# Hybrid DiT block: gated sum kept in its PSUM bank, second norm scaled by a diagonal in the turn, rows left unsplit until their sums

## The chip, the cores and the metric

One Trainium2 chip, one core. The metric is the device time of one execution of the kernel in microseconds (us); the time of a kernel is the median of its runs.

## The reference

One layer of a diffusion backbone on 1024 latent tokens of width 1024 with 256 context tokens, all in fp32. A recurrence branch (HGRN2) and a windowed attention branch read the same normalised input. Then:

```python
def _merge(y_hg, y_at, gates, w_bh, w_ba, w_o):
    g_hg, g_at = jnp.split(gates, 2, axis=-1)
    mixed = jax.nn.sigmoid(g_hg) * (y_hg @ w_bh) + jax.nn.sigmoid(g_at) * (y_at @ w_ba)
    return mixed @ w_o

def _rmsnorm(x, w):
    xf = x.astype(jnp.float32)
    y = xf * lax.rsqrt(jnp.mean(xf * xf, axis=-1, keepdims=True) + EPS)
    return (y * w.astype(jnp.float32)).astype(x.dtype)

def _modulate(x, w, shift, scale):
    return _rmsnorm(x, w) * (1.0 + scale) + shift

def _swiglu(h, w_gate, w_up, w_down):
    return (jax.nn.silu(h @ w_gate) * (h @ w_up)) @ w_down
```

The merged result, times a gate `g1`, is added to the tokens (x); x is normalised a second time (`_modulate`), goes through `_swiglu` with an inner width of 2816, and is added to x once more.

## The kernel before, in words

Large products run as three fp32r matmuls each: an operand is split into a high part (a cast to fp32r on ScalarE) and a low part (the difference, on VectorE), and high x high, high x low, low x high are summed in a PSUM bank of 128x512. All TensorE instructions are issued in program order by a helper (L76 for a matmul, L79 for a transpose); the order on the other engines is a scheduler's.

**Gated sum (L1159 to L1179).** For each of eight channel tiles `ct` the weights are loaded and split (L136, L137) and two gate rows `ga`, `gb` are loaded and put through a sigmoid. For each token half `t` GpSimd multiplies `gb` by the attention branch (L1169), TensorE makes `bh` of 12 matmuls (four k steps of three) in a bank of the two-bank pool `mm`, VectorE multiplies it by `ga` (L1173) and adds `gb` (L1174), both into `ga`, and the result is split into `mx` (L1175 on ScalarE, L1176 on VectorE).

**Out-projection (L1182 to L1197, L1309 to L1323).** Each half of the weights `wop` comes by DMA (L1188), is multiplied by `g1` on GpSimd (L1193), cast on ScalarE (L1194) and its low part made on VectorE (L1195). `project(nh, bs)` runs eight k steps of three matmuls for each block of 128 tokens in `bs`, yields after each step, and VectorE adds the bank to `xn` (L1323). The first half (nh = 0) runs for all eight blocks, then the second half block by block.

**Second norm (L1212 to L1224, L1266 to L1303).** After block b's second half, `second_norm(b)` squares both halves of `xn[b]` on ScalarE with the sum beside it (L1216, the squares land in `xh`), GpSimd adds the two sums, takes the mean and the root (L1219 to L1221), VectorE scales `xn` by it into `xh` (L1223), and SP stores the rows (L1224). `second_norm_t(b)`, "the turn", then transposes the eight 128x128 pieces of `xh` into two banks `tp` (L1279), and ScalarE applies scale and shift into `r` (L1282). It runs inside block b + 1's second projection, after six of its eight k steps (L1330); block 7's runs behind the first product of both FFN chains (L1483). For blocks 0 to 3 the two results are split into the FFN operands HB11 and HB21. For blocks 4 to 7 three differences and sums with the earlier blocks are made, the earlier rows being put together again from their two parts (L1294, L1295, L1300, L1301), and split into HT2, HT3, HB22; `kt` (from `keep`) holds two of the sums for later operands.

**FFN (L1397 on).** Seven products per pair of tiles replace eight (Strassen's scheme with Winograd's sums). `ux` is made in a bank of `mm` for even pairs: first with HB11, later with HT2; `uz` uses HB21. The weights' sums are made on VectorE in between (L1379 to L1386, L1461 to L1464).

Of the kernel before, what the change touches and what calls it, by code (L numbers as in the profile page):

```python
# [9 lines left out]
F32 = mybir.dt.float32  # L10
# [4 lines left out]
ALU = mybir.AluOpType  # L15
# [4 lines left out]
P = 128  # L20
# [23 lines left out]
def tile_hybrid_block(  # L44
# [1114 lines left out]
    for ct in range(KT):  # L1159
# [7 lines left out]
        for t in range(2):  # L1167
            a = slice(t * 512, t * 512 + 512)
            pool.tensor_tensor(gb[:, a], gb[:, a], t2[ct][t], ALU.mult)  # L1169
            mh, ml = mixed(t, 0, ct), mixed(t, 1, ct)  # L1170
            ps = mm_tile(f"bh_{ct}_{t}")
            whole(gemm_ch(ps, w, hg_hi[t], hg_lo[t], 4))
            dve.tensor_tensor(ga[:, a], ga[:, a], ps, ALU.mult)  # L1173
            dve.tensor_tensor(ga[:, a], ga[:, a], gb[:, a], ALU.add)  # L1174
            act.copy(mh, ga[:, a])  # L1175
            dve.tensor_tensor(ml, ga[:, a], mh.bitcast(F32), ALU.subtract)  # L1176
        if ct == 0:
# [32 lines left out]
    xn_d = [dram.tile([P, D], F32, name=f"xn_d{b}") for b in range(NB)]  # L1210

    def second_norm(b):  # L1212
        xh = []
        for u in range(2):
            xt = pt.tile([P, 512], F32, tag="tmp", bufs=4, name=f"xh{b}_{u}")
            act.activation(xt, xn[b][:, u * 512 : u * 512 + 512], AF.Square, accum_out=ss2[:, 2 * b + u : 2 * b + u + 1])  # L1216
            xh.append(xt)
        r = rs2[:, b : b + 1]
        pool.tensor_tensor(r, ss2[:, 2 * b : 2 * b + 1], ss2[:, 2 * b + 1 : 2 * b + 2], ALU.add)  # L1219
        pool.tensor_scalar(r, r, 1.0 / D, EPS, ALU.mult, ALU.add)  # L1220
        pool.tensor_tensor(r, r, mhalf[:, :1], ALU.pow)  # L1221
        for u in range(2):
            dve.tensor_scalar(xh[u], xn[b][:, u * 512 : u * 512 + 512], r, None, ALU.mult)  # L1223
        sp.dma_start(xn_d[b], xn[b])  # L1224
        return xh

# [22 lines left out]


    kept = {}

    def keep(nm, b):
        i = b % 4
        if i % 2 == 0:
            if (nm, i) == (1, 0):
# [8 lines left out]

    def second_norm_t(b, xh):  # L1266
        t, c = b // 4, slice((b % 4) * P, (b % 4) * P + P)
# [3 lines left out]
        if b == 4:  # L1271
            hop_tile(HT2, pn, ("n8", "n9"))
            hop_tile(HT3, pmA, ("a0", "a1"))
            hop_tile(HB22, pmA, ("a2", "a3"))
        dst = [quarter(pt.tile([P, 512], F32, tag="tmp", bufs=4, name=f"r{b}_{u}")) for u in range(2)]
        for u in range(2):
            tp = psF.tile([P, 512], F32, tag="tp", bufs=2, name=f"tp2_{b}_{u}")
            for i in range(4):
                pe.transpose(tp[:, i * P : i * P + P], xh[u][:, i * P : i * P + P], ident)  # L1279
            for i in range(4):  # L1280
# [5 lines left out]
        if t == 0:  # L1286
            return

        def f(o, p):
            return hop[o][p][:, :, c].bitcast(F32)  # L1290

        r12, r22 = dst
        t1, t4 = keep(1, b), keep(4, b)
        dve.tensor_tensor(t1, r12, f(HB11, 0), ALU.subtract)  # L1294
        dve.tensor_tensor(t1, t1, f(HB11, 1), ALU.subtract)  # L1295
        dve.tensor_tensor(t4, r22, t1, ALU.subtract)
        split_h(HT2, t4, c)
        dve.tensor_tensor(r12, r22, r12, ALU.subtract)
        split_h(HT3, r12, c)
        dve.tensor_tensor(t4, f(HB21, 0), t4, ALU.subtract)  # L1300
        dve.tensor_tensor(t4, t4, f(HB21, 1), ALU.add)  # L1301
        split_h(HB22, r22, c)
# [24 lines left out]
    def norm_late(gen):  # L1327

        for i, us in enumerate(gen):
            if i == 5 and late:  # L1330
                second_norm_t(*late.pop(0))
# [162 lines left out]
    for b in range(2, NB):  # L1494
        whole(project(0, (b,)))
    for b in range(NB):
        norm_late(project(1, (b,)))
        late.append((b, second_norm(b)))
# [153 lines left out]
```

## Time and profile before

| | |
|---|---|
| time, median of 3 runs (lowest to highest) | 1693.41 us (1687.12 to 1694.36) |
| profiled execution: its own time | 1698.77 us |
| its span, mean granted TensorE clock | 1697.0 us, 0.981 |
| busy: TensorE, VectorE, ScalarE, GpSimd | 1609.2, 1111.1, 758.7, 284.6 us |

PE is TensorE, PEld its weight loads, DVE VectorE, ACT ScalarE, POOL GpSimd, SP the engine that issues most DMAs. Busy times are sums of instructions with overlaps taken out; a time of one instruction on PE or DVE is longer than the distance between the starts of two that follow each other, since they are pipelined. The granted clock is a share of 2.4 GHz. L1173 is line 1173 of the kernel before; a name like `gt` is a tile, and `gt<-gt,bh` an instruction that writes `gt` from `gt` and `bh`.

### The profile page before, as it was taken

What the parts mean: (1) busy time and instruction counts of PE and PEld (TensorE: products, weight loads), DVE (VectorE), ACT (ScalarE), POOL (GpSimd) and SP (SyncE); (2) the same over time, 40 slices, a digit from 0 to 9 for tenths busy, and PEclk for the clock granted to TensorE, in tenths of its full rate; (3) what the DMA queues carried; (4) which work ended last, traced back from release to release, by engine and by line L of the source; (5) the groups of instructions that cost most, each with busy time, mean ns of one, the idle gap of its engine ahead of it and who ended that gap; (6) DMA issues with size and microseconds to landing.
All of it is one profiled execution on the core that took longest, in us unless ns stands there. A gap on an engine that the chain in (4) does not pass through costs nothing.

```text
span 1697.0 us, 23284 instructions
## 1 busy us (share of the span) xinstructions
PE 1609.2 (95%) x8424; PEld 1341.9 (79%) x8424; DVE 1111.1 (65%) x2018; ACT 758.7 (45%) x1405; POOL 284.6 (17%) x339
## 2 busy tenths in 40 slices
PE   6899999999899999999988997899999999999998
PEld 3689879998777787778877776687888888888887
DVE  3872577777768969696328628877555665646464
ACT  4411345555555565644445247333333333443431
POOL 2402454420012313132114412000000000000000
PEclk9899999999999999999999999899999999999999
DMA  9771312221366566552265414786233222577573
GB/s 361 269 268 52 106 60 69 67 94 54 127 192 202 188 204 202 200 171 93 87 218 183 160 50 149 275 293 219 99 110 126 94 99 100 195 241 239 189 235 123
DMA packets 199468, 274.18 MB, mean 162 GB/s; under 512 B 13775, under 2 KB 115248, under 8 KB 199352
## 3 DMA queue, kind: packets, MB, share of 16 engines
q1 hardware_dynamic: 183800, 250.13, 44.0%
q10 hardware_dynamic: 15552, 22.55, 3.6%
q8 instruction: 66, 1.08, 0.3%
q14 instruction: 50, 0.41, 0.1%
HBM read 192.14 MB, written 80.49 MB: 161 GB/s over the span
## 4 chain that ended last, share of the span: by engine, by line
PE 36%; DMA 5%; DVE 4%; ACT 2%; issue 2%; POOL 1%; SPq 0%; POOLq 0%; ACTq 0%; DVEq 0%
PE ux L76 10%; PE dx L76 7%; PE dy L76 5%; PE uy L76 5%; PE wo L76 3%; PE uz L76 3%; DMA wd<-in_w_ffn_down_dram 2%; PE ba L76 1%; ACT r L1282 1%; PE bh L76 1%; DMA gt<-gates_d 1%; DMA dr<-in_w_ffn_down_dram 1%; DMA wr<-in_w_ffn_up_dram 1%; ACT xh L1216 0%; DVE mx L1176 0%
## 5 line engine op out<-in xcount | busy, mean ns | idle before, releaser
L76 PE MATMUL ux<-hop,op 128*128 128x512 f32 x1032 | 244.2, 394 | 8.6 <-ACT hop L1240 4.4
L76 PEld LDWEIGHTS ux<-hop,op 128*128 128x128 f32 x1032 | 196.5, 191 | 51.1 <-ACT hop L1240 4.8
L1241 DVE TENSOR_TENSOR dp<-dr,dp 128x1024 fp32r<-128x1024 f32 x77 | 93.9, 1223 | 85.1 <-ACT dp L1240 77.6
L1240 ACT CAST dp<-dr 128x1024 fp32r<-128x1024 f32 x77 | 81.0, 1052 | 117.6 <-PE dy L76 49.1
L76 PE MATMUL uy<-hop,op 128*128 128x512 f32 x528 | 123.3, 389 | 0.0
L76 PE MATMUL dx<-dp 128*128 128x512 f32 x528 | 120.6, 389 | 0.6 <-DVE cu L1476 0.6
L76 PEld LDWEIGHTS dx<-dp 128*128 128x128 f32 x528 | 99.0, 188 | 21.6 <-DVE cu L1476 1.0
L76 PEld LDWEIGHTS uy<-hop,op 128*128 128x128 f32 x528 | 99.1, 188 | 20.6
L76 PE MATMUL g<-hhi,whi_g 128*128 128x512 f32 x256 | 110.7, 433 | 2.3 <-ACT gs_g L348 2.3
L76 PE MATMUL g<-hhi,wlo_g 128*128 128x512 f32 x256 | 101.5, 396 | 0.0
L76 PE MATMUL g<-hlo,whi_g 128*128 128x512 f32 x256 | 101.2, 395 | 0.0
L76 PE MATMUL wo<-wop,mx 128*128 128x512 f32 x384 | 90.4, 395 | 0.0
L76 PE MATMUL dy<-dp 128*128 128x512 f32 x396 | 90.2, 389 | 0.0
L76 PEld LDWEIGHTS dy<-dp 128*128 128x128 f32 x396 | 74.3, 188 | 15.4
L1241 DVE TENSOR_TENSOR op<-wr,op 128x512 fp32r<-128x512 f32 x84 | 57.6, 685 | 40.6 <-ACT op L1240 40.5
L76 PEld LDWEIGHTS wo<-wop,mx 128*128 128x128 f32 x384 | 72.4, 190 | 14.8
L1240 ACT CAST op<-wr 128x512 fp32r<-128x512 f32 x84 | 52.1, 623 | 68.0 <-PE ux L76 36.1
L1241 DVE TENSOR_TENSOR op<-ws,op 128x512 fp32r<-128x512 f32 x66 | 45.5, 689 | 42.8 <-ACT op L1240 42.5
L655 DVE CUSTOM_DVE_ANT_0 e<-s,masks,bc 128x640 f32<-128x640 f32 (+1 forms) x64 | 54.2, 848 | 27.1 <-PE s L76 26.8
L660 ACT ACTIVATE e<-e,ngm 128x640 f32<-128x640 f32 (+1 forms) x64 | 51.7, 808 | 38.5 <-DVE ngm L659 38.3
L678 ACT CAST th<-ptp 128x512 fp32r<-128x512 f32 x76 | 43.2, 587 | 45.7 <-PE ptp L79 43.6
L679 DVE TENSOR_TENSOR tl<-ptp,th 128x512 fp32r<-128x512 f32 x76 | 51.1, 687 | 15.2 <-ACT th L678 14.6
(458 smaller groups left out, 3940.1 us busy)
## 6 DMA issues: line engine op xcount, KB each, us to landing
aw<-in_w_ada_dram SPq DMA_DIRECT2D x24, 1024.0 KB, 9.1
dr<-a_d SPq DMA_DIRECT2D x77, 256.0 KB, 4.0
wr<-in_w_ffn_gate_dram SPq DMA_DIRECT2D x11, 1024.0 KB, 5.1
wd<-in_w_ffn_down_dram SPq DMA_DIRECT2D x22, 512.0 KB, 6.7
wr<-in_w_ffn_up_dram SPq DMA_DIRECT2D x11, 1024.0 KB, 6.2
t_d<-td SPq DMA_DIRECT2D x44, 256.0 KB, 2.1
a_d<-cu SPq DMA_DIRECT2D x44, 256.0 KB, 2.6
dr<-t_d SPq DMA_DIRECT2D x44, 256.0 KB
```

Of the source, the lines that this page charges most:

```text
L76: self.chain(nc.tensor.matmul(*a, **k))
L655: dve.tensor_tensor_reduce(e[:, :n], ps[:, LC : LC + n], self.mask, 1.0, sinkb[:, 4 * g + j : 4 * g + j + 1], ALU.add, ALU.max, self.mx[:, ...
L660: tbl(act.activation(e[:, :n], e[:, :n], AF.Exp, bias=self.ngm[:, j : j + 1], accum_out=self.den[:, j : j + 1]))
L678: self.copied = act.copy(th, tp)
L679: dve.tensor_tensor(tl, tp, th.bitcast(F32), ALU.subtract)
L1240: act.copy(hi, src)
L1241: dve.tensor_tensor(lo, src, hi.bitcast(F32), ALU.subtract)
L1282: act.activation(dst[u][:, i], tp[:, i * P : i * P + P], AF.Identity, scale=m2[:, 8 + m : 9 + m], bias=m2[:, m : m + 1])
```

## The change

Three parts. The gated sum runs in place in its bank, which now comes from the four-bank `gu` pool; its split reads the bank. The second norm scales by a matmul: the turn multiplies a piece of `xn` by a diagonal of the reciprocal roots (128x128, `diag`), where it transposed a scaled copy; the first square of a block is issued two blocks behind its first projection (those of blocks 6 and 7 behind the last one), the squares land in `mm` banks, and the turn is hooked one k step later. The turned rows of blocks 0 to 3 are written straight into the kept tiles, unsplit, and the sums of blocks 4 to 7 are made from these in place.

```diff
--- before.py
+++ after.py
@@ -1168,12 +1168,12 @@
             a = slice(t * 512, t * 512 + 512)
             pool.tensor_tensor(gb[:, a], gb[:, a], t2[ct][t], ALU.mult)
             mh, ml = mixed(t, 0, ct), mixed(t, 1, ct)
-            ps = mm_tile(f"bh_{ct}_{t}")
+            ps = psF.tile([P, 512], F32, tag="gu", name=f"bh_{ct}_{t}")
             whole(gemm_ch(ps, w, hg_hi[t], hg_lo[t], 4))
-            dve.tensor_tensor(ga[:, a], ga[:, a], ps, ALU.mult)
-            dve.tensor_tensor(ga[:, a], ga[:, a], gb[:, a], ALU.add)
-            act.copy(mh, ga[:, a])
-            dve.tensor_tensor(ml, ga[:, a], mh.bitcast(F32), ALU.subtract)
+            dve.tensor_tensor(ps, ps, ga[:, a], ALU.mult)
+            dve.tensor_tensor(ps, ps, gb[:, a], ALU.add)
+            act.copy(mh, ps)
+            dve.tensor_tensor(ml, ps, mh.bitcast(F32), ALU.subtract)
         if ct == 0:
             g1 = pt.tile([P, 1024], F32, tag="gg", bufs=1, name="g1")
             sp.dma_start(g1, mod2_d[0, 0:D].partition_broadcast(P))
@@ -1209,20 +1209,21 @@
     rs2 = const.tile([P, NB], F32, name="rs2")
     xn_d = [dram.tile([P, D], F32, name=f"xn_d{b}") for b in range(NB)]
 
+    def square(b, u):
+        act.activation(mm_tile(f"sq{b}_{u}"), xn[b][:, u * 512 : u * 512 + 512], AF.Square,
+                       accum_out=ss2[:, 2 * b + u : 2 * b + u + 1])
+
     def second_norm(b):
-        xh = []
-        for u in range(2):
-            xt = pt.tile([P, 512], F32, tag="tmp", bufs=4, name=f"xh{b}_{u}")
-            act.activation(xt, xn[b][:, u * 512 : u * 512 + 512], AF.Square, accum_out=ss2[:, 2 * b + u : 2 * b + u + 1])
-            xh.append(xt)
+
+        square(b, 1)
         r = rs2[:, b : b + 1]
         pool.tensor_tensor(r, ss2[:, 2 * b : 2 * b + 1], ss2[:, 2 * b + 1 : 2 * b + 2], ALU.add)
         pool.tensor_scalar(r, r, 1.0 / D, EPS, ALU.mult, ALU.add)
         pool.tensor_tensor(r, r, mhalf[:, :1], ALU.pow)
-        for u in range(2):
-            dve.tensor_scalar(xh[u], xn[b][:, u * 512 : u * 512 + 512], r, None, ALU.mult)
+        diag = pt.tile([P, 512], F32, tag="tmp", bufs=4, name=f"diag{b}")[:, :P]
+        dve.tensor_scalar(diag, ident, r, None, ALU.mult)
         sp.dma_start(xn_d[b], xn[b])
-        return xh
+        return diag
 
 
 
@@ -1248,11 +1249,12 @@
...
     kept = {}
 
     def keep(nm, b):
         i = b % 4
-        if i % 2 == 0:
+        if (nm, i) not in kept:
             if (nm, i) == (1, 0):
                 pg = pt.tile([P, 1024], F32, tag="gg", bufs=1, name=f"kt{nm}_{i}")
             elif (nm, i) == (4, 2):
@@ -1263,7 +1265,7 @@
             kept[nm, i + 1] = quarter(pg[:, 512:])
         return kept[nm, i]
 
-    def second_norm_t(b, xh):
+    def second_norm_t(b, diag):
         t, c = b // 4, slice((b % 4) * P, (b % 4) * P + P)
         if b == 0:
             hop_tile(HB11, pmB, ("b0", "b1"))
@@ -1272,11 +1274,15 @@
             hop_tile(HT2, pn, ("n8", "n9"))
             hop_tile(HT3, pmA, ("a0", "a1"))
             hop_tile(HB22, pmA, ("a2", "a3"))
-        dst = [quarter(pt.tile([P, 512], F32, tag="tmp", bufs=4, name=f"r{b}_{u}")) for u in range(2)]
+        t1, t4 = keep(1, b), keep(4, b)
+        dst = (t1, t4)
+        if t:
+            dst = [quarter(pt.tile([P, 512], F32, tag="tmp", bufs=4, name=f"r{b}_{u}")) for u in range(2)]
         for u in range(2):
             tp = psF.tile([P, 512], F32, tag="tp", bufs=2, name=f"tp2_{b}_{u}")
             for i in range(4):
-                pe.transpose(tp[:, i * P : i * P + P], xh[u][:, i * P : i * P + P], ident)
+                m = 4 * u + i
+                pe.matmul(tp[:, i * P : i * P + P], xn[b][:, m * P : m * P + P], diag, start=True, stop=True)
             for i in range(4):
                 m = 4 * u + i
                 act.activation(dst[u][:, i], tp[:, i * P : i * P + P], AF.Identity,
@@ -1285,20 +1291,14 @@
                 split_h((HB11, HB21)[u], dst[u], c)
         if t == 0:
             return
-
-        def f(o, p):
-            return hop[o][p][:, :, c].bitcast(F32)
-
         r12, r22 = dst
-        t1, t4 = keep(1, b), keep(4, b)
-        dve.tensor_tensor(t1, r12, f(HB11, 0), ALU.subtract)
-        dve.tensor_tensor(t1, t1, f(HB11, 1), ALU.subtract)
-        dve.tensor_tensor(t4, r22, t1, ALU.subtract)
-        split_h(HT2, t4, c)
+        t2_ = quarter(pt.tile([P, 512], F32, tag="tmp", bufs=4, name=f"t2_{b}"))
+        dve.tensor_tensor(t1, r12, t1, ALU.subtract)
+        dve.tensor_tensor(t2_, r22, t1, ALU.subtract)
+        split_h(HT2, t2_, c)
         dve.tensor_tensor(r12, r22, r12, ALU.subtract)
         split_h(HT3, r12, c)
-        dve.tensor_tensor(t4, f(HB21, 0), t4, ALU.subtract)
-        dve.tensor_tensor(t4, t4, f(HB21, 1), ALU.add)
+        dve.tensor_tensor(t4, t4, t2_, ALU.subtract)
         split_h(HB22, r22, c)
 
     def late_operands(o, nm):
@@ -1327,7 +1327,7 @@
     def norm_late(gen):
 
         for i, us in enumerate(gen):
-            if i == 5 and late:
+            if i == 6 and late:
                 second_norm_t(*late.pop(0))
 
 
@@ -1493,6 +1493,9 @@
     first_operands()
     for b in range(2, NB):
         whole(project(0, (b,)))
+        square(b - 2, 0)
+    square(NB - 2, 0)
+    square(NB - 1, 0)
     for b in range(NB):
         norm_late(project(1, (b,)))
         late.append((b, second_norm(b)))
```

VectorE, last two channel tiles of the gated sum, where the out-projection's weights (`wop`, L1195) come in between. Lines with - are before, with + after; `bh` is the bank, `gt` the gate rows, `mx` the low part of the split.

```order
 L1195 TENSOR_TENSOR wop_0_9679<-wo_0_9677,wop_0_9679 128x512
-L1173 TENSOR_TENSOR gt_9542<-gt_9542,bh_1_9566 128x512
+L1173 TENSOR_TENSOR bh_1_9566<-bh_1_9566,gt_9542 128x512
+L1176 TENSOR_TENSOR mx_1_1_9294<-bh_0_9548,mx_0_1_9292 128x512
+L1174 TENSOR_TENSOR bh_1_9566<-bh_1_9566,gt_9542 128x512
 L1195 TENSOR_TENSOR wop_0_9679<-wo_0_9677,wop_0_9679 128x512
-L1176 TENSOR_TENSOR mx_1_1_9294<-gt_9542,mx_0_1_9292 128x512
-L1174 TENSOR_TENSOR gt_9542<-gt_9542 128x512
```

The instructions now name the bank `bh` where they named `gt`, and L1176 and L1174 stand ahead of the second L1195 where they stood behind it.

TensorE, from the second half of block 6's turn to the FFN's first product. `tp_6_1` is the turn, `wo_7` block 7's out-projection, `ux_0` the FFN's first product. Before:

```order
L79 MATMUL tp_6_1_10461<-ident,xh_1_10423 128x128 [waits DVE_49,Activation_49]
L79 MATMUL tp_6_1_10461<-ident,xh_1_10423 128x128 x3
L76 MATMUL wo_7_10431<-wop_6_9755,mx_0_1_9296 128x512 x2
L76 MATMUL wo_7_10431<-wop_6_9755,mx_1_1_9298 128x512
L76 MATMUL wo_7_10431<-wop_6_9755,mx_0_1_9296 128x512 x2
L76 MATMUL wo_7_10431<-wop_6_9755,mx_1_1_9298 128x512
L76 MATMUL ux_0_10503<-hop_0_10062,ope_0_9839 128x512
L76 MATMUL ux_0_10503<-hop_1_10063,ope_0_9839 128x512
```

After:

```order
L76 MATMUL tp_6_1_10458<-diag_10422,xn_9722 128x128 [waits Activation_49]
L76 MATMUL tp_6_1_10458<-diag_10422,xn_9722 128x128 x3
L76 MATMUL wo_7_10425<-wop_6_9755,mx_0_1_9296 128x512 x2
L76 MATMUL wo_7_10425<-wop_6_9755,mx_1_1_9298 128x512
L76 MATMUL ux_0_10492<-hop_0_10079,ope_0_9839 128x512 [waits Activation_49]
L76 MATMUL ux_0_10492<-hop_1_10080,ope_0_9839 128x512
```

Three `wo_7` rows stand behind the turn where six stood, and the first `ux_0` has a wait on ScalarE that it had not.

VectorE, from the first sum of the FFN's weights (L1379) on, block 7. `xn_9724` is its residual (L1323), `kt` a kept tile, `hop` an operand's part. Before, up to L1323:

```order
L1379 TENSOR_TENSOR ws_10565<-wr_0_10563 128x512
L1300 TENSOR_TENSOR kt_0_10333<-hop_0_10064,kt_0_10333 128x512
L1294 TENSOR_TENSOR kt_2_10470<-r_0_10450,hop_0_10062 128x512
L1380 TENSOR_TENSOR ws_10565<-ws_10565,wr_0_10563 128x512
L1382 TENSOR_TENSOR wr_0_10563<-wr_0_10563 128x4x128
L1301 TENSOR_TENSOR kt_0_10333<-kt_0_10333,hop_1_10065 128x512
L1295 TENSOR_TENSOR kt_2_10470<-kt_2_10470,hop_1_10063 128x512
L1298 TENSOR_TENSOR r_0_10450<-r_1_10451,r_0_10450 128x512
L1323 TENSOR_TENSOR xn_9724<-xn_9724,wo_7_10431 128x512
```

After, up to block 7's diagonal (L1224 there):

```order
L1379 TENSOR_TENSOR ws_10553<-wr_0_10551 128x512
L1323 TENSOR_TENSOR xn_9724<-xn_9724,wo_7_10425 128x512
L1242 TENSOR_TENSOR hop_1_10607<-kt_0_10084,hop_0_10606 128x4x128
L1296 TENSOR_TENSOR kt_2_10197<-r_0_10447,kt_2_10197 128x512
L1242 TENSOR_TENSOR hop_1_10607<-kt_0_10084,hop_0_10606 128x4x128
L1380 TENSOR_TENSOR ws_10553<-ws_10553,wr_0_10551 128x512
L1382 TENSOR_TENSOR wr_0_10551<-wr_0_10551 128x4x128
L1297 TENSOR_TENSOR t_6_10467<-r_1_10448,kt_2_10197 128x512
L1299 TENSOR_TENSOR r_0_10447<-r_1_10448,r_0_10447 128x512
L1242 TENSOR_TENSOR hop_1_10316<-r_1_10448,hop_0_10315 128x4x128
L1224 TENSOR_SCALAR diag_10487<-ident,rs_9763 128x128
```

The residual stands second where it stood ninth. Before, 44 instructions stand from L1379 to the low part of block 7's HT2; after, 35.

## Rows read from the trace of the kernel before

**Rows 1.** Windows by stage: length, busy PE, PEld, DVE, ACT, POOL, clock, DMA share, GB/s.

```profile
919.60:938.50 18.90, 12.19 (x50) 8.87 (x49) 18.35 (x18) 10.13 (x15) 15.73 (x11) 1.00 0.61 192
938.50:991.40 52.90, 52.90 (x235) 43.80 (x235) 26.53 (x34) 11.09 (x20) 15.11 (x13) 1.00 0.34 113
991.40:1030.20 38.80, 33.61 (x169) 27.12 (x168) 16.99 (x29) 26.39 (x72) 7.25 (x15) 1.00 0.17 68
1030.20:1067.70 37.50, 24.20 (x98) 19.08 (x96) 35.92 (x62) 26.11 (x58) 6.48 (x6) 0.84 0.47 162
1075.00:1483.00 408.00, 405.70 (x1782) 335.13 (x1780) 266.09 (x414) 152.55 (x257) 0.00 (x0) 1.00 0.46 159
```

**Rows 2.** Waits of PE, 886 to 1075 us: us in total, times, longest.

```profile
PE tp L79 <- DVE xh L1223: 12.0, 7, 4.5
PE bh L76 <- DVE gt L1173: 6.7, 4, 2.7
PE ux L76 <- ACT hop L1240: 4.4, 1, 4.4
```

**Rows 3.** Timeline of PE: start, us, instruction [idle before <-releaser]; the branch and output products.

```profile
887.17 0.62 PE L76 MATMUL bh<-yh_s,whi_bh 128*128 128x512 f32 x2
...
938.55 53.21 PE L76 MATMUL wo<-wop,mx 128*128 128x512 f32 x234
```

**Rows 4.** Timeline of DVE, 917 to 948 us: first, last but one, last.

```profile
917.28 1.77 DVE L137 TENSOR_TENSOR wlo_bh<-wraw_bh,whi_bh 128x512 fp32r<-128x512 f32 x1
...
946.15 0.68 DVE L1195 TENSOR_TENSOR wop<-wo,wop 128x512 fp32r<-128x512 f32 x1
946.75 1.78 DVE L1176 TENSOR_TENSOR mx<-gt,mx 128x512 fp32r<-128x512 f32 x1
```

**Rows 5.** Tile gt: ns min/median/max, first and last start, form.

```profile
L1173 DVE TENSOR_TENSOR gt<-gt,bh x16: 672/677/689, 890.1 to 943.6; 128x512 f32<-128x512 f32 x16
L1174 DVE TENSOR_TENSOR gt<-gt x16: 676/684/1773, 890.9 to 944.3; 128x512 f32<-128x512 f32 x16
```

**Rows 6.** Windows of line L1195 alone: us, DVE busy (x count), clock, DMA share, GB/s.

```profile
917.28:948.54 31.26, 9.14 (x8) 1.00 0.62 198
```

**Rows 7.** Timeline of PE, 999 to 1068 us: turns of the second norm and the tail.

```profile
999.20 1.06 PE L79 MATMUL tp<-ident,xh 128*128 128x128 f32 x8 [1.11 <-DVE xh L1223]
1000.02 5.72 PE L76 MATMUL wo<-wop,mx 128*128 128x512 f32 x24
1006.82 1.06 PE L79 MATMUL tp<-ident,xh 128*128 128x128 f32 x8 [1.08 <-DVE xh L1223]
...
1030.26 5.71 PE L76 MATMUL wo<-wop,mx 128*128 128x512 f32 x24
...
1067.73 7.85 PE L76 MATMUL ux<-hop,op 128*128 128x512 f32 x23 [2.17 <-DVE hop L1241]
```

**Rows 8.** Timeline of PE, 541.8 to 542.5 us: plain fp32 products of 128x128, then another.

```profile
541.83 0.61 PE L76 MATMUL o<-q,s 128*128 128x128 f32 x4
542.27 0.39 PE L76 MATMUL o<-sc,v 128*128 128x128 f32 x2
542.41 0.48 PE L76 MATMUL gh<-hhi,whi_gh 128*128 128x512 f32 x1
```

**Rows 9.** Timeline of all engines, 999 to 1007 us: one block's chain.

```profile
999.87 2.91 ACT L1282 ACTIVATE r<-tp,vt 128x128 f32<-128x128 f32 x8 [2.47 <-PE tp L79]
...
1002.62 0.67 ACT L1216 ACTIVATE xh<-xn 128x512 f32<-128x512 f32 x1
...
1004.59 0.19 POOL L1219 TENSOR_TENSOR rs<-ss 128x1 f32<-128x1 f32 x1 [6.06 <-ACT xh L1216]
...
1006.19 0.88 DVE L1223 TENSOR_SCALAR xh<-xn,rs 128x512 f32<-128x512 f32 x2 [0.44 <-POOL rs L1221]
```

**Rows 10.** Timeline of DVE, 1031 to 1075 us: the last block's scaling.

```profile
1051.62 0.88 DVE L1223 TENSOR_SCALAR xh<-xn,rs 128x512 f32<-128x512 f32 x2 [1.00 <-POOL rs L1221]
```

**Rows 11.** Chain that ended last, 1030 to 1070 us: start, us, what.

```profile
1034.42 5.26 DMA wr<-in_w_ffn_gate_dram
```

## Prediction

> **What bounds the kernel now.** I read the windows by stage first. Behind the stages that the change touches TensorE is busy 405.70 of 408 us [rows 1]: nothing else can end that stretch sooner, and work removed from VectorE there is worth nothing. A gain has to come from 886 to 1075 us, where the table shows four kinds of stretch. From 919.6 to 938.5 us TensorE works 12.19 of 18.90 us while VectorE works 18.35. From 938.5 to 991.4 us TensorE is full. From 991.4 to 1030.2 us neither is full (33.61 and 16.99 of 38.80): a chain of dependences paces them. From 1030.2 to 1067.7 us VectorE is full again (35.92 of 37.50) while TensorE works 24.20.
>
> The list of waits puts names to it [rows 2]: 12.0 us in seven turns (the transposes of the second norm) that wait for the scaled rows of L1223, 6.7 us in four waits of the branch products `bh` for a bank that L1173 still reads, and 4.4 us in one wait of the first FFN product for `hop`. Together 23.1 us.
>
> **Part 1, the gated sum.** TensorE starts its last branch product stage at 887.17 us and reaches the out-projection at 938.55 [rows 3]. By the pitch of that row, 53.21 us for 234 matmuls with about 0.17 of tail, one takes 0.2267 us. Eight channel tiles of 24 matmuls are 43.5 us, to 930.7; 7.8 us are lost, 6.7 of them in the four waits for a bank. There are two banks before, four after.
>
> Why L1173 is late: VectorE runs without a gap from 917.28 to the last split at 946.75 [rows 4], 31.2 us with that split's 1.78. An instruction costs 0.60 us from start to start (0.68 recorded), but some cost 1.77: L137 at 917.28, L1176 at 946.75. All of these have both inputs in SBUF, and GpSimd is busy 15.73 of the 18.90 us there [rows 1]. The tile's rows show the same: L1174, both inputs in SBUF, reaches 1773 ns; L1173, which reads a bank, never passes 689 [rows 5]. After the change L1173, L1174 and L1176 each read a bank. So I take 0.60 for each: of the 29 instructions of that stretch 20 are such (12.0 us); the eight L1195 keep what they took before, 9.14 in sum [rows 6], and L137 its 1.77. That is 22.9 us in place of 31.2, and with four banks TensorE waits for none of it; I keep one stall of 0.8 us at the first out-projection weights, which are cast, multiplied and split on other engines. Gain 7.0 us; bounds 0 (the weights pace it) and 7.8 (all that was lost); nearest is the upper, since the waits name L1173 and not the weights.
>
> Here a rule speaks against the change. L1173 with a PSUM input has a median of 677 ns, L1174 without one 684 [rows 5]: reading a bank costs nothing that shows; writing one is not shown. The Trainium skill (Perfetto Trace Analysis, Optimizing Scalar/DVE Operations) gives VectorE about 60 ns of access overhead per instruction on SBUF and about 125 ns on PSUM. By it 32 in-place instructions would be 32 x 0.065 = 2.1 us longer (an estimate from that page), and the time at most 1681.4. The row disagrees for reads; I go by the row.
>
> **Part 2, the turn.** Before, a turn is eight transposes at one record each, 0.82 us (1006.82 to the next products), and the period of a block is 1006.82 - 999.20 = 7.62, with 24 matmuls at 0.2267 = 5.44, the turn 0.82 and a wait of 1.1 [rows 7]. After, it is eight plain fp32 matmuls against a diagonal of 128x128. The program's other plain fp32 matmuls of this size show two records each: six records from 541.83 to 542.41, 0.097 each [rows 8]. Sixteen are 1.6 us, so the turn grows by 0.8.
>
> What shrinks is the chain behind the wait. Before: eight L1282 from 999.87, two squares of 0.67 from 1002.62 with a cast between, GpSimd's three steps from 1004.59, two 128x512 scalings from 1006.19, the turn [rows 9]. After, one square is issued long before, among the first projection's 52.90 us, where ScalarE is busy 11.09 [rows 1]: eight more at 0.7 have room, cost nothing, and would cost 5.6 if they hadn't. The scaling becomes one 128x128. Two 128x512 scalings take 0.88 us [rows 10], the second 0.4 after the first; the new one has a quarter of the elements of one, so it lies between 0 and 0.5, and I take 0.2. Chain after: first half of the turn 0.8 and its landing 0.26, L1288 2.75, cast 0.52, square with its sum 0.70, GpSimd 1.60, diagonal 0.2, issue 0.14: 7.0. TensorE's own work per block: 1.6 + 5.44 = 7.04. The two balance.
>
> The turn also moves behind three more matmuls of the next block. The order shows it for block 6: three `wo_7` rows after its turn where six stood. That gives the chain 0.68 us more, so a small lateness is covered.
>
> Call K0 the start of block 7's second projection. It stands six matmuls after 1030.26 [rows 7], 1031.62, which is 93.07 us after the out-projection starts. After: 360 matmuls 81.6, six turns 9.6, and 0.3 for a first wait: 91.5. Gain 1.5; bounds +3 (turn at 1.3) and -3 (chain at 8).
>
> **Part 3, the operands in place.** For blocks 4 to 7 VectorE loses two instructions each, and two scalings of every block become one small one. What counts is the tail after K0. There the chain of waits goes from a weight DMA that lands at 1039.68, K0 + 8.06, into L1379 [rows 11], and then along VectorE, instruction by instruction, to the split (L1241) on which TensorE goes on at 1067.73, K0 + 36.11 [rows 7]. In between stand 44 instructions at 0.60 and one wait of 1.00 for GpSimd's root [rows 10]. After, the order puts block 7's add second instead of ninth, and its diagonal eleventh, where the first scaling stood nineteenth; 24 instructions follow up to the split. K0 + 8.1 + 10 x 0.602 = 14.1, +1.0 for GpSimd, +0.2 = 15.3; 24 x 0.602 and the split's 0.74 bring it to K0 + 30.5. Gain 5.6; bounds 0 (GpSimd's root takes as long again as its wait shows, and the queue shifts) and 8.
>
> Two waits are new: `ux_0` of both chains takes a bank last written by the squares of blocks 6 and 7 (the order shows the wait on ScalarE). Behind them the whole TensorE queue stands. The square of block 7 is ready at about K0 + 10.1 (add after L1379, 0.7, square 0.7, plus ScalarE's queue), TensorE needs it at K0 + 9.8: 0.3 us, hidden while VectorE sets the end at K0 + 30.5. The store of the rows is issued at the same place on SP, and GpSimd keeps its three steps. After the tail TensorE is full, so what is left of the gain arrives whole. The granted clock there (0.84 on the mean, so in part the lower level [rows 1]) I leave as it is.
>
> **Sum.** 7.0 + 1.5 + 5.6 = 14.1 us. The profiled execution took 1698.77 us, 5.4 above the median of 1693.41; it becomes 1684.7, and the median 1679.3. About 0.5%, 8.5 us, is what a measurement of this kernel can tell.
>
> **Rivals.**
> (a) The out-projection's weights pace the start instead, along DMA, GpSimd, cast and split. The seventh k step's are split at 946.15 [rows 4] and so ready at 946.8; its products come 36 matmuls after 938.55, at 946.7. If GpSimd doesn't get faster when VectorE does, starting sooner only waits there. Then part 1 is worth 0: 1686.3. For it: no slack in those rows. Against: VectorE, not GpSimd, is the one without gaps. Chance 0.18.
> (b) The diagonal turn costs four times the old one, 3.2 us. Then K0 comes 81.6 + 19.2 = 100.8 after the start, part 2 is -7.7, the sum 4.9: 1688.5. The two records a matmul of [rows 8] speak against it. Chance 0.1. The Trainium skill (TensorE: Matmul & The Clock Gate, Terms) has the transpose mode four times faster for fp32; by it this rival holds, and the trace's records, twice as many and no longer each, disagree.
> (c) Slower. An instruction that reads and writes a bank in place costs VectorE what the longest L1174 did, 1.78, in place of 0.60. Then a channel tile has four of these (7.12) and L1176 twice and L137 once at 0.60 (1.80): 8.9 us against TensorE's 5.44. Eight tiles from 890, where the first L1173 can start three us behind 887.17, are 71 us, the eight L1195 9.15: 970. The out-projection needs all but the last tile's second half, some 4 us less: it starts near 966, 27 later than before, and parts 2 and 3 keep 7.1: 1693.4 + 27 - 7.1, about 1713. The loss outweighs parts 2 and 3 from 1.15 us each: 8 x (4 x 1.15 + 1.8) + 9.15 - 4 is 56, from 890 to 946. No row shows a write to a bank by this instruction; the reads at 677 ns [rows 5] speak against. Chance 0.05.
> (d) One wait only replaces another in part 3, GpSimd's root coming as late against VectorE's queue as before: part 3 gives 0, 1684.9, and with part 2 at its lower end 1689.4. Chance 0.1.
> (e) More than forecast: with shorter waits before it, TensorE's clock stays at its upper level where 23 products now take 7.85 us [rows 7]; at 0.2267 each they take 5.2. That is 2.6 us more: 1676.7, and with the upper bounds of parts 1 and 2 1674.4. Chance 0.07.
>
> **Numbers.** Forecast 0.5. The range runs from 1673 (case e with the upper bounds, and 1.4 of part 3's 2.4) to 1691 (rival b, or d at its lower end, and the spread of the runs); it leaves out (c) and what has no case. Faster by over 0.5% means below 1684.9: the forecast, (e), a part of (a): 0.61. Slower by over 0.5%: (c) and mishaps like it, 0.07. The rest 0.32.
>
> **What would show it.** Part 1: no `bh` wait on L1173, its three lines all at 0.6 to 0.7, the out-projection starting near 931.5. Part 2: 128 records of the turn, 1.6 us each turn, a period near 7.0. Part 3: block 7's turn near K0 + 15, HT2's product near K0 + 30.5. Wrong would be: L1174 above 1 us, a period over 7.6, or VectorE with gaps in the tail.

## The result, and the profile after

The change took 1683.38 us (median of nine) where the kernel before took 1691.96 (nine): ratio 0.9946, 95% interval 0.9933 to 0.9958. A second measurement of the same kernel gave 0.9933 (0.9919 to 0.9947). So it is faster by 0.5 to 0.7%, 9 to 11 us, where 14.1 were forecast; the time lies inside the range of 1673 to 1691. The profiled execution took 1687.67 us (span 1685.8), 11.1 below the one before and 4.3 above its own median.

The windows of the change over the stretches that answer to those of [rows 1] (length, busy PE, PEld, DVE, ACT, POOL, clock, DMA share, GB/s): branch products, first half of the output projection, turns, tail, and the 100 us behind it.

```profile
886.70:930.60 43.90, 43.70 (x193) 35.85 (x191) 34.77 (x52) 23.03 (x34) 19.50 (x15) 1.00 0.63 210
930.60:986.70 56.10, 54.35 (x237) 44.41 (x238) 24.25 (x35) 17.35 (x37) 16.51 (x15) 1.00 0.35 113
986.70:1025.80 39.10, 39.10 (x220) 33.41 (x220) 14.72 (x25) 24.59 (x65) 7.70 (x15) 1.00 0.17 67
1025.80:1055.60 29.80, 21.25 (x107) 16.97 (x105) 27.93 (x48) 24.58 (x52) 3.93 (x6) 0.95 0.50 168
1062.60:1162.60 100.00, 96.99 (x416) 79.69 (x416) 76.84 (x124) 34.17 (x60) 0.00 (x0) 0.97 0.85 296
```

TensorE is full in the branch products and in the turns now (39.10 of 39.10, against 33.61 of 38.80 before). The tail's window is 29.80 us long; that of [rows 1], 37.50, begins 1.4 us ahead of K0 (the start of block 7's second projection), so the tail is 6.3 us shorter. VectorE is still nearly full in it (27.93 of 29.80). The list of TensorE's waits from 880 to 1075 us, which answers to [rows 2]:

```profile
PE ux L76 <- DVE hop L1242: 4.3, 1, 4.3
PE ux L76 <- ACT hop L1241: 3.3, 1, 3.3
PE wo L76 <- DVE wop L1195: 1.7, 1, 1.7
PE tp L76 <- DVE diag L1224: 1.0, 1, 1.0
PE wo L76 <- DVE mx L1176: 0.3, 1, 0.3
```

The 6.7 us of `bh` and all but one of the seven turns' waits are gone; a wait for the output weights is new. TensorE's timeline shows where (start, us, instruction, idle before):

```profile
930.66 4.19 PE L76 MATMUL wo<-wop,mx 128*128 128x512 f32 x16 [0.26 <-DVE mx L1176]
936.54 50.39 PE L76 MATMUL wo<-wop,mx 128*128 128x512 f32 x221 [1.68 <-DVE wop L1195]
986.76 1.95 PE L76 MATMUL tp<-diag,xn 128*128 128x128 f32 x16
988.47 5.70 PE L76 MATMUL wo<-wop,mx 128*128 128x512 f32 x24
994.00 2.00 PE L76 MATMUL tp<-diag,xn 128*128 128x128 f32 x16
...
1025.11 5.73 PE L76 MATMUL wo<-wop,mx 128*128 128x512 f32 x24
...
1033.41 5.62 PE L76 MATMUL ux<-hop,ope 128*128 128x512 f32 x24
1040.05 2.05 PE L76 MATMUL tp<-diag,xn 128*128 128x128 f32 x16 [1.02 <-DVE diag L1224]
...
1055.65 7.16 PE L76 MATMUL ux<-hop,op 128*128 128x512 f32 x23 [4.27 <-DVE hop L1242]
```

From the first branch product, at 886.72, to the first output product are 43.94 us (before 51.38). The sixteenth output product should end 3.63 us later; the seventeenth starts after 5.88: a stall of 2.25 us. A turn takes 1.7 to 1.8 us; the periods of the blocks run from 7.24 to 7.52. K0, three products behind 1025.11, is 1025.79; the product that ends the tail starts at K0 + 29.86 (before K0 + 36.11).

The bank's tile answers to [rows 5] (ns min/median/max, first and last start, form):

```profile
L1173 DVE TENSOR_TENSOR bh<-bh,gt x16: 681/694/700, 889.6 to 933.7; 128x512 f32<-128x512 f32 x16
L1174 DVE TENSOR_TENSOR bh<-bh,gt x16: 680/691/700, 890.4 to 936.4; 128x512 f32<-128x512 f32 x16
L1175 ACT CAST mx<-bh x16: 566/575/588, 891.2 to 938.2; 128x512 fp32r<-128x512 f32 x16
L1176 DVE TENSOR_TENSOR mx<-bh,mx x16: 674/692/694, 891.8 to 938.9; 128x512 fp32r<-128x512 f32 x16
```

None of VectorE's three lines passes 700 ns; before, L1174 reached 1773 and L1176 1781.

### The profile page after: what moved, and what is told of

The parts are those of the page before. It is cut to its first block, busy times and chain, and to the rows that moved or that the text cites. A ratio compares the mean times of both kernels' runs of the same rounds, so it can differ in the third digit from the quotient of the medians.

```text
span 1685.8 us, 23376 instructions
## 1 busy us (share of the span) xinstructions
PE 1612.7 (96%) x8488; PEld 1347.1 (80%) x8488; DVE 1089.5 (65%) x2002; ACT 760.7 (45%) x1405; POOL 278.3 (17%) x339
## 4 chain that ended last, share of the span: by engine, by line
PE 43%; DMA 3%; DVE 3%; issue 1%; ACT 1%; SPq 0%; DVEq 0%; ACTq 0%
PE ux L76 13%; PE dx L76 7%; PE uy L76 6%; PE dy L76 5%; PE wo L76 5%; PE uz L76 3%; PE bh L76 2%; DMA wr<-in_w_ffn_up_dram 1%; PE ba L76 1%; PE tp L76 1%; DMA wd<-in_w_ffn_down_dram 1%; DMA a_d<-cu 0%; DVE wop L1195 0%; DVE op L1242 0%; DMA gt<-gates_d 0%
## 5 line engine op out<-in xcount | busy, mean ns | idle before, releaser
L1241 ACT CAST op<-ws 128x512 fp32r<-128x512 f32 x66 | 41.1, 623 | 44.3 <-PE uz L76 26.1
```

Source lines behind the costliest of these rows:

```text
L1241: act.copy(hi, src)
```

## The experiments

For every kernel the same three stretches were read from TensorE's timeline: A, first branch product to first output product; B, from there to the FFN's first product (`ux`); C, from there to the first `uy`, the product with HT3. W is the wait behind the tail of `ux` for L1407's copy (below). All are in us, from the one profiled execution of each kernel; the ratio is to the kernel before, from all its runs.

| kernel | A | B | C | A+B+C | W | ratio (95%) |
|---|---|---|---|---|---|---|
| before | 51.38 | 103.56 | 33.31 | 188.25 | 2.1 | 1 |
| the change | 43.94 | 102.75 | 29.23 | 175.92 | 3.0 | 0.9946 (0.9933 to 0.9958) |
| part 1 alone | 43.63 | 105.68 | 33.32 | 182.63 | 0.5 | 0.9971 (0.9959 to 0.9982) |
| part 2 alone | 52.07 | 100.14 | 35.76 | 187.97 | 1.8 | 1.0004 (0.9988 to 1.0020) |
| part 3 alone | 51.78 | 103.09 | 30.92 | 185.79 | 0 | 0.9972 (0.9958 to 0.9986) |
| two banks | 63.62 | 100.37 | 29.13 | 193.12 | 2.4 | 1.0020 (1.0008 to 1.0033) |
| sum in SBUF | 45.16 | 108.99 | 30.03 | 184.18 | 1.7 | 0.9979 (0.9967 to 0.9991) |
| three passes | 43.52 | 100.31 | 29.08 | 172.91 | 3.4 | 0.9936 (0.9918 to 0.9954) |
| transposes in 0 to 3 | 43.52 | 100.70 | 28.65 | 172.87 | 0.4 | 0.9919 (0.9899 to 0.9939) |
| both of these | 44.11 | 99.13 | 29.50 | 172.74 | 1.3 | 0.9893 (0.9875 to 0.9912) |
| turn a step earlier | 43.52 | 103.47 | 29.44 | 176.43 | 0 | 0.9914 (0.9898 to 0.9930) |
| transposes in all | 43.61 | 101.07 | 28.14 | 172.82 | 1.6 | 0.9901 (0.9886 to 0.9916) |
| the change again | 43.52 | 104.67 | 28.91 | 177.10 | 3.0 | 0.9933 (0.9919 to 0.9947) |
| transposes in all, three passes | 43.52 | 99.07 | 28.94 | 171.53 | 0.4 | 0.9884 (0.9865 to 0.9903) |

The two profiles of the change differ by 1.9 us in B and 0.4 elsewhere. The 1.9 lie in the stall: from the first output product to block 0's turn they have 56.10 and 58.07 us, from that turn to K0 39.03 and 38.98. So a difference below 2 us in B, or between two ratios whose intervals overlap, is not read; one between turns is.

C has to be read with care: `ux` starts 7.5 to 7.6 us behind K0 where the turn is hooked late, 10.5 before, and 12.3 with part 3 alone. So the tail is compared by its length from K0 to the product that ends it: before 36.1, part 1 alone 36.1, part 2 alone 35.4, part 3 alone 35.0, the change 29.9 and 29.4, transposes in 0 to 3 29.5, transposes in all 28.6.

### The parts, one at a time

Part 1 alone puts the diff's first hunk into the kernel before.

> Part 1 alone (gated sum in place in four banks; second norm as before). If the parts add up, as the forecast has it: first branch product to first output product 44 us (before 51.4, the whole change 44.0), then one stall of some 2 us at the output weights inside the 93 us up to block 7's second projection (95.3), and the tail as before (36.1): a net gain of 5 us, near 1687. If VectorE's backlog only moves into the output projection (rival a), the stretch up to block 7's second projection grows by the whole 7 us and the time is that of before within 1 us.

The parts add up here: A is 43.63, C is that of before, and the stall inside B shows as two waits of 0.46 and 0.92 for L1195. The forecast's sum for part 1 was 7.0; it is worth 5.6 by the stretches and 4.9 by the ratio.

Part 2 alone leaves the gated sum and the old sums of the rows as they were.

> Part 2 alone (diagonal in the turn, first square early, hook one step later; gated sum and sums of the rows as before). If the turn only trades TensorE's time against the wait: from the first output product to block 7's second projection 92.9 us (before 93.1), turns of 1.75 us and no wait before them; the tail loses the two scalings' 0.7 us and part of GpSimd's wait, 1 to 3 us of 36.1. Net gain 1 to 3 us. If most of the tail's 6 us comes from the diagonal and not from the sums in place, the tail is 30 to 31 us and the gain 5 to 6.

B falls by 3.4 us and C rises by 2.5, both mostly because `ux` starts earlier; up to K0 0.5 us are gained and from K0 0.7. The time is that of before: on its own part 2 is worth nothing that shows.

Part 3 alone keeps the transposes of scaled rows.

> Part 3 alone (rows of blocks 0 to 3 kept unsplit, sums in place; transposes of scaled rows as before). If the tail's gain is that of VectorE's missing instructions: 8 of 128x512 at 0.60 of which those of blocks 6 and 7 and a half of block 5's lie in the tail, 3 to 5 us, tail 31 to 33 us; the stretch up to block 7's second projection unchanged at 93 us. If the tail's gain needs the diagonal (the add of block 7 issued earlier), the tail is 35 to 36 us and the gain under 1 us.

C falls by 2.4, but 1.8 of that is the later start of `ux`; from K0 the tail is 35.0 us, the second side of the expectation. Up to K0, which neither side expected to move, 2.2 us are gained: the first turns follow each other without a wait.

```profile
994.95 1.06 PE L79 MATMUL tp<-ident,xh 128*128 128x128 f32 x8
...
1001.51 1.06 PE L79 MATMUL tp<-ident,xh 128*128 128x128 f32 x8
...
1024.02 1.06 PE L79 MATMUL tp<-ident,xh 128*128 128x128 f32 x8 [2.41 <-DVE xh L1223]
...
1034.17 1.94 PE L79 MATMUL tp<-ident,xh 128*128 128x128 f32 x8 [3.61 <-DVE xh L1223]
```

The four periods from block 0's turn to block 4's sum to 26.7 us (before 30.5), the next two to 19.1 (before 16.2). In the short ones one square stands between a block's add and GpSimd's first step, where two stood before, though no edit of this run moves a square.

To see why parts 2 and 3 need each other in the tail, here is VectorE's busy time from the tail's first sum of weights (the `ws` that waits for the DMA) to the start of the product that ends the tail, in this order: before, part 2 alone, part 3 alone, the change (length, busy and count, clock, DMA share, GB/s), one fence for each kernel.

```profile
1039.71:1067.73 28.02, 26.97 (x46) 0.80 0.43 151
```

```profile
1036.12:1063.54 27.42, 26.90 (x46) 0.85 0.50 162
```

```profile
1034.33:1061.16 26.83, 22.02 (x38) 0.75 0.34 117
```

```profile
1033.69:1055.65 21.96, 21.49 (x37) 0.93 0.44 144
```

With part 2 alone block 7's turn is early, but VectorE has the same 46 instructions and works through all of them. With part 3 alone it has 38, but stands still for 4.8 us, 3.6 of them before these three, which wait for GpSimd's root, for a row of the late turn and for the product behind that turn:

```profile
1047.14 0.88 DVE L1223 TENSOR_SCALAR xh<-xn,rs 128x512 f32<-128x512 f32 x2 [1.00 <-POOL rs L1221]
1050.43 0.69 DVE L1293 TENSOR_TENSOR kt<-r,kt 128x512 f32<-128x512 f32 x1 [0.61 <-ACT r L1285]
1054.40 0.69 DVE L1409 TENSOR_TENSOR cg<-uz,cg 128x512 f32<-128x512 f32 x1 [1.95 <-PE uz L76]
```

Only with both is the queue short and nearly without gaps: this stretch loses 0.6 and 1.2 us with one part alone, 6.1 with both.

### Banks or read ports

```diff
-            ps = psF.tile([P, 512], F32, tag="gu", name=f"bh_{ct}_{t}")
+            ps = mm_tile(f"bh_{ct}_{t}")
```

> The whole change, but the gated sum's bank from the old pool of two. A bank is now held through multiply, add, cast and split, some 3 us, where TensorE fills the other in 2.72: if the four banks are what makes room, first branch product to first output product is 47 to 55 us against 44.0 with four, and 3 to 11 us of the time go. If only the missing slow instructions count, it stays at 44 to 45 us and the time that of the change.

A is 63.62 us, more than either side expected, 12 us above the kernel before; the list of waits names the split (L1176), up to which the bank is now held:

```profile
PE bh L76 <- DVE mx L1176: 12.1, 9, 3.5
```

The waits are 12.1 of the 19.7 us that A is longer than in the change. The rest is a lower granted clock, 0.92 over A where the change has 1.00: TensorE is busy 51.4 us with the products that take 43.7 there.

The other half: four banks, but the sum in SBUF.

```diff
-            dve.tensor_tensor(ps, ps, ga[:, a], ALU.mult)
-            dve.tensor_tensor(ps, ps, gb[:, a], ALU.add)
-            act.copy(mh, ps)
-            dve.tensor_tensor(ml, ps, mh.bitcast(F32), ALU.subtract)
+            dve.tensor_tensor(ga[:, a], ga[:, a], ps, ALU.mult)
+            dve.tensor_tensor(ga[:, a], ga[:, a], gb[:, a], ALU.add)
+            act.copy(mh, ga[:, a])
+            dve.tensor_tensor(ml, ga[:, a], mh.bitcast(F32), ALU.subtract)
```

> The whole change, but the gated sum goes to SBUF as before (multiply and add write the gate rows, split reads them) while the bank still comes from the pool of four. If the gain of part 1 is the four banks: first branch product to first output product 44 to 45 us and the time that of the change within 1 us. If it is that VectorE's instructions read a bank and so never take 1.77 us: L1174 and L1176 again reach 1.77 us; four banks hide most of it from the branch products, but VectorE's backlog holds the output weights and the last splits, and the stall behind the first output products grows from 2.2 us to 5 to 8; the time is 3 to 6 us above the change's.

Its gate tile has the long instructions again, and its waits stand behind the first output products:

```profile
L1174 DVE TENSOR_TENSOR gt<-gt x16: 675/686/1779, 886.3 to 940.2; 128x512 f32<-128x512 f32 x16
```

```profile
PE wo L76 <- DVE wop L1195: 3.4, 1, 3.4
PE wo L76 <- ACT wop L1194: 2.6, 1, 2.6
PE wo L76 <- DVE gt L1173: 1.5, 1, 1.5
```

Four banks hide the backlog from the branch products (A 45.16) and hand it on: B is 4.3 to 6.2 us longer than in the change. Part 1 needs both of its halves.

### The stall behind the first output products

```diff
-        for ks in (range(KT - 2), range(KT - 2, KT)):
+        for ks in (range(KT - 4), range(KT - 4, KT - 2), range(KT - 2, KT)):
```

> The whole change, with the first two output blocks in three passes over the k steps (0 to 3, 4 to 5, 6 to 7) in place of two (0 to 5, 6 to 7), so that the sixth step's weights are needed after 27 products and not after 15. They are split at 936.5 where the products start at 930.7. If their arrival is what the stall of 2.2 us is: it shrinks to under 0.5, the rest is unchanged, gain 2 us over the change. If the whole chain of weights paces the stretch (rival a), the stall moves to steps 6 and 7 with the same 2 us.

No wait of TensorE is listed from 884 to 1026 us, and the output products run on from the first one:

```profile
927.59 17.62 PE L76 MATMUL wo<-wop,mx 128*128 128x512 f32 x77
```

B is 2.4 us shorter than the change's: the stall was the arrival of two steps' weights, not the pace of the whole chain. The ratio (0.9936) can't be told from the change's; B varies by nearly as much between two profiles of the change.

### The diagonal

```diff
+        if b < 4:
+            xh = []
+            for u in range(2):
+                xt = pt.tile([P, 512], F32, tag="tmp", bufs=4, name=f"xh{b}_{u}")
+                dve.tensor_scalar(xt, xn[b][:, u * 512 : u * 512 + 512], r, None, ALU.mult)
+                xh.append(xt)
+            sp.dma_start(xn_d[b], xn[b])
+            return xh
...
+                if b < 4:
+                    pe.transpose(tp[:, i * P : i * P + P], diag[u][:, i * P : i * P + P], ident)
+                else:
```

> The whole change, but blocks 0 to 3 are turned by transposes of scaled rows as before (their first square still early, their results still written to the kept tiles), blocks 4 to 7 by the diagonal. If the diagonal costs TensorE 0.93 us a turn and the scaled rows are ready in time there: periods of 6.3 us in place of 7.3 for four blocks, 3.5 to 4 us gained over the change. If the chain behind the turn bounds the period at about 7, as the forecast has it, a wait of 0.6 us appears before each transpose and only 1 us is gained.

The periods of these blocks are 7.0 us, with a wait before each turn but the first:

```profile
990.07 1.06 PE L79 MATMUL tp<-ident,xh 128*128 128x128 f32 x8 [0.49 <-DVE xh L1227]
...
997.07 1.06 PE L79 MATMUL tp<-ident,xh 128*128 128x128 f32 x8 [0.47 <-DVE xh L1227]
```

The chain behind the turn is the bound there, the second side. B gains 2.0 us, not 3.7, and only 1.4 of that lie between block 0's turn and K0.

Then with the three passes:

> The three passes over the k steps and the transposes in blocks 0 to 3 together. If both are what they look like: 2 + 3.7 us below the change, ratio to before near 0.991. If the tail waits for VectorE at a fixed time (the weight DMA that opens its sums), what is gained ahead of it is lost again there: ratio 0.994 to 0.995.

0.9893: what is gained ahead of the tail is kept (B 99.13, C 29.50).

The same with `b < 8`, that is transposes in all eight blocks:

> The change with transposes of scaled rows in all eight blocks (first square early, sums in place): as the run with transposes in blocks 0 to 3, but for blocks 4 to 7. If the diagonal pays where VectorE is the bound: VectorE gets 1.0 us a block back for blocks 6 and 7, and a fifth tile stands against four buffers in blocks 4 to 7, so the tail (first FFN product to its third bank's) is 31 to 34 us against 28.7, and the time 2 to 5 us above that run. If the diagonal is worth nothing anywhere, tail and time are those of that run.

The first side was wrong. The tail does not grow (C 28.14, and 28.6 us from K0), and the time can't be told from that of transposes in four blocks. Two rows of one turn (scaling, transposes) show how little the scaled rows cost:

```profile
1002.78 0.88 DVE L1227 TENSOR_SCALAR xh<-xn,rs 128x512 f32<-128x512 f32 x2 [0.44 <-POOL rs L1222]
...
1003.41 1.06 PE L79 MATMUL tp<-ident,xh 128*128 128x128 f32 x8 [0.47 <-DVE xh L1227]
```

In the tail VectorE's first scaling stands where the diagonal stood, 6.6 us behind the opening sum (6.0 in the change), and up to the ending product it has 36 instructions in 20.79 us. The diagonal pays in no stage. What part 2 brings to the tail (28.6 us from K0 here, 35.0 with part 3 alone) is in its other edits: the early square, the bank in which it lands, and the later hook. These three were not run apart with transposes; with the diagonal the later hook is not what makes the tail short (next run).

In blocks 0 to 3 the early square brings nothing beyond part 3 alone: four periods of 28.0 us here, 26.7 there. The difference lies in GpSimd's last step, 1.01 us here, where a split of VectorE runs beside it, and 0.55 in three of the four periods there, where none does (two fences, here and part 3 alone):

```profile
1001.64 0.69 DVE L1250 TENSOR_TENSOR hop<-kt,hop 128x512 fp32r<-128x512 f32 x1 [0.44 <-ACT hop L1249]
1001.73 1.01 POOL L1222 TENSOR_TENSOR rs<-rs,mhalf 128x1 f32<-128x1 f32 x1
```

```profile
1000.29 0.55 POOL L1221 TENSOR_TENSOR rs<-rs,mhalf 128x1 f32<-128x1 f32 x1
```

### The place of the turn

```diff
-            if i == 6 and late:
+            if i == 5 and late:
```

> The whole change, with the turn back behind six of the next block's eight k steps. The chain from one turn to the next runs over ScalarE (2.75 us of scale and shift, then the square) and doesn't start at the products, and TensorE's own 7.2 us a block are longer than it: periods of 7.2 to 7.3 as in the change, no waits before the turns, the time that of the change within 1 us. If the later place is what covers the chain: a wait of 0.4 to 0.7 us before each of six turns, 3 to 4 us lost.

The sum of A, B and C is that of the change within what its two profiles differ (176.43 against 175.92 and 177.10), and from K0 the tail is 29.9 us. The turns of blocks 5 and 6 come late, with idle times of 0.5 and 0.6 before them, so that the two periods up to block 6's turn take 16.1 us where they take 15.0: the second side holds for two of the six turns. The ratio of 0.9914 was not expected. The stretches don't hold it; what comes behind the tail does: from the first `uy` to the end of the span 617.2 us, against 623.2 in both profiles of the change, where TensorE waits 3.0 (W) and runs slowly behind that ("Behind the tail", below). That the hook's place causes this, and not merely the moment at which the tail ends, is not shown.

### The change again, and the best of the parts

> The change itself once more, for a second profile and a tighter ratio: 0.993 to 0.996, with the same stage times within 0.5 us up to the end of the tail; what differs between two profiles of one kernel lies outside.

The ratio is 0.9933. A and C agree within 0.5, B does not (1.9), so the stall is not the same from one execution to the next.

Transposes in all blocks and three passes, the change's other edits kept:

> Transposes of scaled rows in all eight blocks and the three passes over the k steps, on top of the change's gated sum, early square and sums in place. If the diagonal is worth nothing anywhere and the stall behind the first output products is the weights': no wait between the first output product and the second block's turn, periods of 7.0, tail of 28 us, 2 us below the run with transposes alone, ratio 0.988 to 0.990. If the tail waits for VectorE at a fixed time, what the passes gain is lost there and the ratio stays at 0.990 to 0.991.

1672.56 us where before took 1692.78, ratio 0.9884: 1.2%, about twice the change's gain. Against the run with both edits and the diagonal in blocks 4 to 7 (0.9893) it can't be told apart. A wait of 0.39 us for the new squares' bank and 7.5 us before transposes, 4.4 of them ahead of `ux`, are left in it.

## Why the prediction was right, and where it was off

**Part 1: mechanism right, one term too small.** L1173, L1174 and L1176 cost what the forecast took, 0.60 from start to start, and the slow instructions left. (VectorE was not wholly without a gap before: at 921.79 us it had waited 0.45 for a cast. No sum changes by it.) The part was sized at 7.0 with one stall of 0.8 at the weights; A gained 7.4, the stall was 2.25, so 5.2. The forecast had the weights' stall as a term and sized it too small, so rival (a) was true for a third of the part. Writing the bank in place costs VectorE 7 ns on L1174 (684 to 691) and 17 on L1173 (677 to 694). The Trainium skill (Perfetto Trace Analysis, Optimizing Scalar/DVE Operations) gives some 65 ns more for an instruction of VectorE on PSUM than on SBUF; the trace disagrees, and decides. The same section's figures for ScalarE, about 93 ns on SBUF and 51 on PSUM, agree in their difference: L1175 fell from 620 to 575 ns when it began to read the bank.

**Part 2: sized at 1.5, worth 0.2.** The turn takes 1.7 to 1.8 us, not 1.6, in the two records a matmul that the forecast read; rival (b) with 3.2 us is out. Old turn to new, 0.82 to 1.75, is a factor of 2.1. The Trainium skill (TensorE: Matmul & The Clock Gate, Terms) has the transpose mode four times faster for fp32; here it is not.

From the first output product to K0 there are 95.13 us, 92.88 without the stall, against 93.07 before. The forecast said that chain and TensorE would balance at 7.0 us a block; they nearly do in blocks 0 to 3, at 7.24 to 7.30. In the chain the square with its sum took 0.84 where the forecast had 0.70, and the diagonal with its issue 0.42 where it had 0.34; the turns were each 0.1 to 0.2 longer.

The step that failed is what the forecast compared. It credited the diagonal with shortening the chain, and never set it against transposes with the early square. The diagonal lengthens the chain: its first half delays ScalarE by 1.12 us (the forecast's own 1.06), where four transposes take 0.67, and on VectorE it saves only 0.2 (0.43 from the diagonal's start to the turn, 0.63 from the first scaling's). With transposes and the early square the period is 7.0.

**Part 3 with the tail: sized at 5.6, worth 6.2.** K0 + 30.5 was forecast and K0 + 29.86 measured; block 7's turn came at K0 + 14.3 where 15.3 were forecast, since VectorE did not have to wait for GpSimd's root, for which the forecast kept 1.0. The forecast counted the fewer instructions and the earlier turn in one queue, and so got the sum right; as two parts alone they are worth under a third of it (0.7 and 1.2 us from K0).

**Behind the tail: "the gain arrives whole" failed.** The three parts sum to 11.6 us by the stretches, 2.5 less than forecast: 1.8 of that is missing in part 1 and 1.3 in part 2, and part 3 gave 0.6 more. The chain that ended last in the change shows where TensorE stops once more (the window ends at 1106 us and cuts the last row):

```profile
1093.19 7.19 DMA a_d<-cu
...
1100.54 0.60 ACT cu L1407
...
1101.18 5.06 PE ux L76 x11
```

The store of `cu` (SP's queue, with the loads and the other stores, the DMA engines busy at 0.85 in these 100 us) frees the tile late, L1407 waits for it, and `ux` for L1407's bank: 3.0 us, where a wait of the same kind, named as the store of `td`, took 2.1 before.

The wait costs more than its length. The 12 products behind it ran at a granted clock of 0.50, the lower of the two levels (1.2 of 2.4 GHz). They took 5.28 us where 12 take 2.72 at the upper level. Before, they took 4.44 at 0.62 (one fence each: the change, before; length, busy PE, PEld, DVE, ACT, POOL, clock, DMA share, GB/s).

```profile
1101.18:1106.46 5.28, 5.28 (x12) 4.12 (x13) 3.06 (x5) 0.95 (x2) 0.00 (x0) 0.50 0.97 317
```

```profile
1151.10:1155.54 4.44, 4.44 (x13) 3.49 (x14) 4.09 (x7) 1.99 (x4) 0.00 (x0) 0.62 0.68 259
```

The clock does not fall behind every such wait: in the run with three passes 12 products behind a wait of 3.4 us took 2.85. Why it falls in one and not in the other is not shown.

With this the profiled executions add up. From the first `uy` to the end of the span there are 621.6 us before, 623.2 in both profiles of the change, and 617.2 and 617.4 in the two kernels with no such wait (the earlier turn, part 3 alone). So of the 12.3 us that A, B and C gain, 1.6 are lost behind the tail, 0.5 were gained ahead of A, and the span fell by 11.2. This is one execution of each kernel; the nine of the change range from 1677.8 to 1687.7 us.

Rival (c), the slower one, is out by the rows of the bank's tile, and (d), no gain in part 3, by the tail's 29.9 us from K0. The granted clock of the tail rose to 0.95 from 0.84, and the 23 products behind it took 7.16 us, not 7.85: a quarter of case (e). Two errors the other way hid some of what parts 1 and 2 missed: the 0.6 us of part 3, and these 0.7, which the forecast left out of its sum.

## What to carry to other kernels

Two edits on one queue can be worth under two us apart and six together: a shorter queue needs its inputs earlier, and earlier inputs need a shorter queue; run each alone before crediting either. Before replacing a copy by a product with a diagonal, forecast the same edit without it: here the diagonal doubled the turn on an engine that became full, and transposes with the other edits kept did at least as well. A sum made in place in PSUM frees VectorE of its slow double SBUF reads, but holds the bank through the whole chain, so it needs banks for that chain's length (four here; two cost more than the slow reads).

## What the runs showed of the hardware that was not expected

VectorE writes a PSUM bank in place at the pace of SBUF: 691 to 694 ns against 677 to 684. An instruction with both inputs in SBUF reaches 1.78 us beside GpSimd's work, and L1173, L1174 and L1176 with one input in a bank never passed 0.70 in 48 instances. Before, one split runs at 0.69 while GpSimd stands idle, and the next, 1.2 us later and beside GpSimd's product, is that of 1.78 at 946.75 [rows 4] (two fences, VectorE and GpSimd):

```profile
945.54 0.69 DVE L1176 TENSOR_TENSOR mx<-gt,mx 128x512 fp32r<-128x512 f32 x1
```

```profile
946.29 3.39 POOL L1193 TENSOR_TENSOR wo<-wo,g 128x512 f32<-128x512 f32 x2 [5.00 <-DVE mx L1176]
```

It goes both ways: GpSimd's root on 128x1 takes 1.01 us beside a split of VectorE and 0.55 alone. ScalarE's cast from a bank is 45 ns shorter than from SBUF (575 and 620).
